# Two block sums of the up weights by an adding load instead of two VectorE additions

## The chip, the cores and the metric

The kernel runs on one core of a Trainium2 chip. The core has five engines with a queue of instructions each: TensorE (PE; its weight loads are listed as PEld), VectorE (DVE), ScalarE (ACT), GpSimd (POOL) and SyncE (SP), which here only issues loads and stores. Semaphores order the engines among each other; the transfers themselves run on 16 DMA engines. The metric is the time of one execution on the device, in microseconds.

## The reference, cut to what matters

Two layers, each with a mixing part (attention, convolution and RWKV heads) and an MLP, on 512 positions of width 1024 in float32. The change touches the MLP alone:

```python
h = rms_norm(x, norm_mlp_g[l])                                        # (512, 1024)
x = x + jnp.square(jax.nn.relu(h @ w_mlp_up[l])) @ w_mlp_down[l]      # up 1024 -> 4096, down 4096 -> 1024
```

## The kernel before

**Layout.** All activations lie transposed: `x[j]` is a tile of 128 features by 512 positions, j from 0 to 7. Weights lie in device memory as groups of 128 output columns, each a row of 8 blocks of 128x128; half a group, four blocks, is 128x512 floats, 256 KB, and is what one load brings.

**Precision.** Float32 products are made of three matmuls: each operand is split into a high part (a cast to `fp32r`, on ACT) and a low part (operand less high part, on DVE or POOL), and high x high, high x low and low x high are added in PSUM. So every weight block that goes into a matmul costs one cast and one subtraction first.

**The up products.** The 32 groups of up columns are treated in two ways. The first four (`N_ONE`) go one by one through `up`: eight blocks, 24 matmuls of 512 positions. Three of the four are written into the order by hand that ends the mixing part (`products`, under `manual_schedule`). The other 28 are taken in pairs (`two(i0, i1)`, 14 pairs a layer): the product of a 2x2 block matrix (two groups by two halves of the 1024 features) with a 2x2 block matrix of activations (two halves of the features by two halves of the positions, H = 256) is made with seven block products instead of eight, after Winograd. With w11, w12 the halves of group i0 and w21, w22 those of group i1, the weights of the seven products p1 to p7 are w11, w12, s4 = w12 - s2, w22, s1 = w21 + w22, s2 = s1 - w11 and s3 = w11 - w21. Each product is four blocks, 12 matmuls of 256 positions (`product`); the order on PE is p1, p5, p6, p2, p7, p3, p4. They gather in three PSUM tiles, `pa`, `pb` and `pc`. The activations' own differences are made once a layer by `blocks(q)`, q from 0 to 3, from the activations times gain (`bn`, made by `by_gain`), and split into `thi` and `tlo`.

The block sums are made by `sum_` on DVE from raw loads (`raw`, tag `sraw`, six buffers; SyncE issues them). In the first pair of a layer s1 and s3 are made with a form that also adds a column of zeros (`none`), which holds them back until the last activation is there. `both` casts (ACT) and subtracts (DVE) into five buffers `shi` and `slo`, so that weights can be made up to five products ahead of PE.

**After the products.** PSUM parts are copied or added into `p1`, `p5`, `u2`, `c1`, `c0`. `square` takes the larger of a value and 0 times the norm's factor `rs` (DVE, into a tile `r`), squares it (ACT, into `m`), and `kept` splits `m` into `mh` and `ml`, the inputs of the down products; `ml` is made on POOL from the fifth on. Ten buffers (`RING`) hold them.

**The down products** come in half groups, `down(h, js)`: four output tiles of 12 matmuls of 512 positions each, added into `x` by DVE. One such call follows nearly each pair; between the second and the third pair of a layer there is none. The weights come through `weights`, with four sets of buffers (three in `wp`, one in `fp`).

**Order.** Behind the hand-written order of the mixing part the instructions are placed by a scheduler that goes by the order of the program and by the times that it assumes, with a queue in order for each engine. So a load may be issued well ahead of its place in the text. At the end of the mixing part (`inner_norm`) POOL raises the mean square to -1/2 (L371, `rrf`), PE spreads it over the partitions (`prbf`), and ACT copies it into `rsf`, the factor `rs` of the squares.

At the start of the MLP part the program runs `up(0)` to `up(3)`, `by_gain(0)` to `by_gain(7)`, `down(0, range(4))`, `blocks(0)` to `blocks(3)`, and then the 14 pairs with the other down products. Before the change POOL issues no DMA at all.

Of the kernel before, what the change touches and what calls it, by code (L numbers as in the profile page):

```python
# [22 lines left out]
S = 512  # L23
# [248 lines left out]
def tile_trunk(ctx: ExitStack, tc: tile.TileContext, xT, wts, prm_d, cst_d, lora_d, gup_d, lam_d, fin_d, hd_d, out):  # L272
# [293 lines left out]
    for l in range(L):  # L566
# [826 lines left out]
        with ExitStack() as mx:  # L1393
# [17 lines left out]
            def square(cs, name):  # L1411

                r = fp.tile([P, S], F32, tag="r", bufs=2, name=f"r{name}")
                for i, c in enumerate(cs):
                    q = slice(i * H, i * H + c.shape[1])
                    dve.scalar_tensor_tensor(r[:, q], c, 0.0, rs[:, q], ALU.max, ALU.mult)
                m = fp.tile([P, S], F32, tag="m", bufs=3, name=f"m{name}")
                act.activation(m, r, AF.Square)
                kept(m)
# [26 lines left out]
            def blocks(q):  # L1446
                hi, lo = th[q] = [fp.tile([P, 4, H], F32R, tag=f"t{p}{q}", name=f"t{p}{l}_{q}") for p in ("hi", "lo")]
                for i in range(2):
                    u = slice(2 * i, 2 * i + 2)
                    t = fp.tile([P, 2, H], F32, tag="c0" if q == 1 else ("s3", "s4")[i], bufs=1 + (q == 1), name=f"t{l}_{q}_{i}")  # L1450
                    for k in (2 * i, 2 * i + 1):
                        b1, b2, o = bn[k], bn[k + 4], t[:, k % 2]
                        if q == 0:
                            dve.tensor_tensor(o, b1[:, 1], b1[:, 0], ALU.subtract)
                        elif q == 1:
                            dve.tensor_tensor(o, b2[:, 1], tb[0, i][:, k % 2], ALU.subtract)
                        elif q == 2:
                            dve.tensor_tensor(o, b2[:, 1], b1[:, 1], ALU.subtract)
                        else:
                            dve.tensor_tensor(o, b2[:, 0], tb[1, i][:, k % 2], ALU.subtract)  # L1460
                    tb[q, i] = t
                    act.copy(hi[:, u], t)
                    dve.tensor_tensor(lo[:, u], t, hi[:, u].bitcast(F32), ALU.subtract)

            def two(i0, i1):
# [4 lines left out]
                def raw(i, a):  # L1470
                    t = fp.tile([P, 4, P], F32, tag="sraw", bufs=6, name=f"raw{n}_{i}_{a}")
                    nc.sync.dma_start(t.rearrange("p k c -> p (k c)"), wts[wg + i, :, a * P:(a + 4) * P])
                    return t
# [7 lines left out]
                def sum_(name, a, b, op):  # L1481
                    t = fp.tile([P, 4, P], F32, tag=name, name=f"{name}{n}")
                    if i0 == N_ONE and name in ("s1", "s3"):
                        dve.scalar_tensor_tensor(t, a, none, b, ALU.add, op)
                    else:
                        dve.tensor_tensor(t, a, b, op)
                    return t
# [22 lines left out]
                w21 = raw(i1, 0)  # L1510
                w22 = raw(i1, 4)
                s1 = sum_("s1", w21, w22, ALU.add)
# [3 lines left out]
                s2 = sum_("s2", s1, w11, ALU.subtract)  # L1516
# [3 lines left out]
                w12 = raw(i0, 4)  # L1520
                product(pc, both(w12, "p2"), blk(1, 0))
                dve.tensor_tensor(c0[:, :H], pc, p1, ALU.add)
                s3 = sum_("s3", w11, w21, ALU.subtract)
                product(pa, both(s3, "p7"), smm(2), False)
# [3 lines left out]
                s4 = sum_("s4", w12, s2, ALU.subtract)  # L1528
# [4 lines left out]
                square([pa, c1], f"{n}_1")  # L1533
# [25 lines left out]
            for i in range(N_ONE):  # L1559
                up(i)  # L1560
            for j in range(NK):
                by_gain(j)
# [83 lines left out]
```

## Time and profile before

| what | us |
|---|---|
| three timed runs: lowest, median, highest | 1236.31, 1236.34, 1236.89 |
| the profiled execution | 1238.42 |
| its span, first to last instruction | 1236.6 |
| busy: PE, DVE, ACT, POOL | 1226.2, 934.4, 693.0, 351.7 |

The page lists an instruction group as line, engine, operation, written tile and read tiles, shape, and count; then the busy time and the mean in nanoseconds, and the idle time of the engine ahead of it with what ended it. `L285` is the matmul helper for nearly all products, so a group of PE is told by its tile: `pa`, `pb`, `pc` belong to the pairs, `dn` to the down products, `up` to the single up products, `po` to the output projection that ends the mixing part, `prbf` to the norm. `raw<-wts` are the weight loads. In other views a row begins with its start in microseconds from the start of the span. `SPq` means SyncE's queue. PE's clock was granted in full over the whole span but for its last microseconds.

The MLP part of layer 0 begins at 278.64 us with the first `up` matmul, that of layer 1 just behind 886.5 us, where the last `po` matmul ends.

### The profile page before, as it was taken

How to read it: one execution, taken by the hardware profiler on the slowest of the kernel's cores; microseconds unless marked ns; L12 is line 12 of the kernel's file. 1: busy time of each engine (PE TensorE's matmuls, PEld its weight loads, DVE VectorE, ACT ScalarE, POOL GpSimd, SP SyncE). 2: the span in 40 equal slices, each digit the busy share in tenths (PEclk: the TensorE clock that was granted, in tenths of full speed). 3: DMA queues.
4: the chain of work that ended last, by engine and by line, in shares of the span. 5: the costliest groups of instructions: out<-in, count | busy, mean ns of one | idle time of the engine just before them, and what ended most of it. 6: DMA issues, size and time to landing. Idle time of an engine off the chain costs nothing.

```text
span 1236.6 us, 25555 instructions
## 1 busy us (share of the span) xinstructions
PE 1226.2 (99%) x9730; PEld 1056.4 (85%) x9730; DVE 934.4 (76%) x1805; ACT 693.0 (56%) x1456; POOL 351.7 (28%) x450
## 2 busy tenths in 40 slices
PE   9999999999999999999999999999999999999997
PEld 7788788888999998989888888888889999998987
DVE  6787888879887676765666777887798867676753
ACT  6785655558455454544465657464775545454542
POOL 2263636341122111120035455464202211111111
PEclk9999999999999999999999999999999999999999
DMA  6523323124433323321235243232433333323121
GB/s 217 165 91 96 111 90 111 54 86 154 143 97 102 103 94 107 99 86 44 69 105 166 77 126 114 88 85 70 152 113 118 106 102 102 104 95 107 55 69 68
DMA packets 84266, 127.94 MB, mean 103 GB/s; under 512 B 21296, under 2 KB 25136, under 8 KB 84144
## 3 DMA queue, kind: packets, MB, share of 16 engines
q1 hardware_dynamic: 83424, 125.57, 32.5%
q8 instruction: 76, 1.25, 0.4%
q10 hardware_dynamic: 720, 0.75, 0.2%
q14 instruction: 46, 0.38, 0.1%
HBM read 117.11 MB, written 9.18 MB: 102 GB/s over the span
## 4 chain that ended last, share of the span: by engine, by line
PE 92%; DVE 2%; ACT 2%; DMA 1%; POOL 1%; issue 1%; SPq 0%; POOLq 0%; ACTq 0%; DVEq 0%
PE dn L285 25%; PE pj L285 21%; PE pa L285 13%; PE po L285 8%; PE pb L285 7%; PE dnF L285 4%; PE pc L285 3%; PE up L285 2%; PE sc L285 1%; PE ptt L290 1%; PE pg L285 1%; PE pyy L285 1%; PE pzw L285 1%; PE pst L285 1%; DMA raw<-wts 0%
## 5 line engine op out<-in xcount | busy, mean ns | idle before, releaser
L1408 POOL TENSOR_TENSOR ml<-m,mh 128x512 fp32r<-128x512 f32 x56 | 90.5, 1634 | 497.5 <-ACT mh L1407 356.5
L285 PE MATMUL dn<-mh,whi 128*128 128x512 f32 x448 | 175.5, 392 | 0.0
L285 PE MATMUL dn<-ml,whi 128*128 128x512 f32 x448 | 175.2, 391 | 0.1
L285 PE MATMUL dn<-mh,wlo 128*128 128x512 f32 x448 | 175.2, 391 | 0.0
L692 POOL TENSOR_TENSOR wlo<-raw,whi 128x512 fp32r<-128x512 f32 x84 | 111.5, 1328 | 210.4 <-ACT whi L680 167.2
L346 ACT CAST whi<-raw 128x512 fp32r<-128x512 f32 x126 | 77.9, 619 | 157.5 <-PE dn L285 147.8
L285 PE MATMUL pj<-ahim,whi 128*128 128x512 f32 x392 | 156.8, 400 | 0.0
L285 PE MATMUL pj<-ahim,wlo 128*128 128x512 f32 x392 | 156.4, 399 | 0.0
L285 PE MATMUL pj<-alom,whi 128*128 128x512 f32 x392 | 155.9, 398 | 0.0
L1554 DVE TENSOR_TENSOR x<-dn,x 128x512 f32<-128x512 f32 x108 | 74.5, 690 | 89.9 <-PE dn L285 89.8
L680 ACT CAST whi<-raw 128x512 fp32r<-128x512 f32 x142 | 87.7, 618 | 71.7 <-PE pj L285 27.5
L1477 ACT CAST shi_p<-s 128x512 fp32r<-128x512 f32 x112 | 69.4, 621 | 78.4 <-PE pa L285 61.9
L347 DVE TENSOR_TENSOR wlo<-raw,whi 128x512 fp32r<-128x512 f32 x126 | 97.3, 774 | 6.1 <-ACT whi L346 6.1
L285 PEld LDWEIGHTS dn<-mh,wlo 128*128 128x128 f32 x448 | 84.2, 188 | 18.5
L285 PEld LDWEIGHTS dn<-ml,whi 128*128 128x128 f32 x448 | 84.2, 188 | 17.7 <-DVE ml L1408 0.5
L285 PEld LDWEIGHTS dn<-mh,whi 128*128 128x128 f32 x448 | 84.1, 188 | 17.4
L285 PE MATMUL pa<-thi,shi_p 128*128 128x256 f32 x336 | 95.1, 283 | 0.0
L285 PE MATMUL pa<-tlo,shi_p 128*128 128x256 f32 x336 | 94.9, 282 | 0.0
L285 PE MATMUL pa<-thi,slo_p 128*128 128x256 f32 x336 | 94.1, 280 | 0.0
L1478 DVE TENSOR_TENSOR slo_p<-s,shi_p 128x512 fp32r<-128x512 f32 x112 | 77.6, 697 | 21.2 <-ACT shi_p L1477 18.4
L285 PEld LDWEIGHTS pj<-alom,whi 128*128 128x128 f32 x392 | 73.9, 188 | 14.0 <-issue 0.5
L285 PEld LDWEIGHTS pj<-ahim,wlo 128*128 128x128 f32 x392 | 73.8, 188 | 13.9 <-issue 0.2
(427 smaller groups left out, 3242.5 us busy)
## 6 DMA issues: line engine op xcount, KB each, us to landing
raw<-wts SPq DMA_DIRECT2D x389, 256.0 KB, 2.6
qs<-dqhi SPq DMA_DIRECT2D x24, 128.0 KB, 3.4
ks<-dkhi SPq DMA_DIRECT2D x24, 128.0 KB, 3.6
x<-xT SPq DMA_DIRECT2D x8, 256.0 KB, 5.0
dqhi<-qhi SPq DMA_DIRECT2D x6, 256.0 KB, 3.4
dqlo<-qlo SPq DMA_DIRECT2D x6, 256.0 KB, 3.4
dkhi<-khi SPq DMA_DIRECT2D x6, 256.0 KB, 3.1
dklo<-klo SPq DMA_DIRECT2D x6, 256.0 KB, 3.5
```

The source lines that it names most:

```text
L285: ins = nc.tensor.matmul(*a, **k)
L290: ins = nc.tensor.transpose(*a, **k)
L346: act.copy(hi[:, :n], raw[:, :n])
L347: (pool if a and lean[0] else dve).tensor_tensor(lo[:, :n], raw[:, :n], hi[:, :n].bitcast(F32), ALU.subtract)
L680: yield act.copy(hi[:, k0:k1], raw[:, k0:k1])
L692: yield eng.tensor_tensor(lo[:, k0:k1], raw[:, k0:k1], hi[:, k0:k1].bitcast(F32), ALU.subtract)
L1408: (dve if i < 4 else pool).tensor_tensor(lo, m, hi.bitcast(F32), ALU.subtract)
L1477: act.copy(hi, src)
L1478: dve.tensor_tensor(lo, src, hi.bitcast(F32), ALU.subtract)
L1554: dve.tensor_tensor(x[j], pt, x[j], ALU.add)
```

## The change

- For each pair s1 and s3 come from DMA: a new helper `summed(p, name)` has SyncE load one half group into the tile and POOL issue a second load into the same tile that adds to what is there (`accum_op=ALU.add`). It is called for pair p + 1 in the middle of pair p, and for pair 0 behind `up(3)` and ahead of `by_gain`. The tiles `s1` and `s3` have two buffers each instead of one.
- An adding load can only add, so the signs are arranged for it: s1 = w21 + w22 as before, s3 = w21 + w11, s2 = s1 + w11, s4 = w12 + s2. The differences of the activations in `blocks` change sign to match, for q = 1 and q = 3 with `scalar_tensor_tensor` in place of `tensor_tensor`.
- The second output of a pair comes out with its sign turned; `square` takes the smaller of it and 0 (`ALU.min`), and squaring removes the sign.
- w21 isn't loaded by itself any more. The load buffers `sraw` go from six to five.
- `square` writes into `m` and squares in place; the two tiles `r` go, and `m` has four buffers instead of three.
- `sum_` loses the form with `none`.

```diff
-            def square(cs, name):
-
-                r = fp.tile([P, S], F32, tag="r", bufs=2, name=f"r{name}")
+            def square(cs, name, side=ALU.max):
+
+                m = fp.tile([P, S], F32, tag="m", bufs=4, name=f"m{name}")
                 for i, c in enumerate(cs):
                     q = slice(i * H, i * H + c.shape[1])
-                    dve.scalar_tensor_tensor(r[:, q], c, 0.0, rs[:, q], ALU.max, ALU.mult)
-                m = fp.tile([P, S], F32, tag="m", bufs=3, name=f"m{name}")
-                act.activation(m, r, AF.Square)
+                    dve.scalar_tensor_tensor(m[:, q], c, 0.0, rs[:, q], side, ALU.mult)
+                act.activation(m, m, AF.Square)
                 kept(m)
...
-                    t = fp.tile([P, 2, H], F32, tag="c0" if q == 1 else ("s3", "s4")[i], bufs=1 + (q == 1), name=f"t{l}_{q}_{i}")
+                    tag, bufs = ("c0", 2) if q == 1 else (("s3", 2), ("s4", 1))[i]
+                    t = fp.tile([P, 2, H], F32, tag=tag, bufs=bufs, name=f"t{l}_{q}_{i}")
...
                         if q == 0:
-                            dve.tensor_tensor(o, b1[:, 1], b1[:, 0], ALU.subtract)
+                            dve.tensor_tensor(o, b1[:, 0], b1[:, 1], ALU.subtract)
                         elif q == 1:
-                            dve.tensor_tensor(o, b2[:, 1], tb[0, i][:, k % 2], ALU.subtract)
+                            dve.scalar_tensor_tensor(o, tb[0, i][:, k % 2], -1.0, b2[:, 1], ALU.mult, ALU.subtract)
...
                         else:
-                            dve.tensor_tensor(o, b2[:, 0], tb[1, i][:, k % 2], ALU.subtract)
+                            dve.scalar_tensor_tensor(o, tb[1, i][:, k % 2], -1.0, b2[:, 0], ALU.mult, ALU.subtract)
...
+            sums = {}
+
+            def summed(p, name):
+
+                if p < N_TWO:
+                    i0, i1 = N_ONE + p, N_ONE + N_TWO + p
+                    t = sums[p, name] = fp.tile([P, 4, P], F32, tag=name, bufs=2, name=f"{name}{l}_{i0}")
+                    of = [wts[wbase + NG_IN + NG_OUT + i, :, a * P:(a + 4) * P] for i, a in ((i1, 0), (i1, 4) if name == "s1" else (i0, 0))]
+                    nc.sync.dma_start(t.rearrange("p k c -> p (k c)"), of[0])
+                    pool.dma_start(t.rearrange("p k c -> p (k c)"), of[1], accum_op=ALU.add)
+
             def two(i0, i1):
...
-                    t = fp.tile([P, 4, P], F32, tag="sraw", bufs=6, name=f"raw{n}_{i}_{a}")
+                    t = fp.tile([P, 4, P], F32, tag="sraw", bufs=5, name=f"raw{n}_{i}_{a}")
...
-                    if i0 == N_ONE and name in ("s1", "s3"):
-                        dve.scalar_tensor_tensor(t, a, none, b, ALU.add, op)
-                    else:
-                        dve.tensor_tensor(t, a, b, op)
+                    dve.tensor_tensor(t, a, b, op)
...
-                w21 = raw(i1, 0)
-                w22 = raw(i1, 4)
-                s1 = sum_("s1", w21, w22, ALU.add)
+                s1 = sums[i0 - N_ONE, "s1"]
...
-                s2 = sum_("s2", s1, w11, ALU.subtract)
+                s2 = sum_("s2", s1, w11, ALU.add)
...
                 w12 = raw(i0, 4)
+                w22 = raw(i1, 4)
+                for s in ("s1", "s3"):
+                    summed(i0 - N_ONE + 1, s)
...
-                s3 = sum_("s3", w11, w21, ALU.subtract)
-                product(pa, both(s3, "p7"), smm(2), False)
+                product(pa, both(sums[i0 - N_ONE, "s3"], "p7"), smm(2), False)
...
-                s4 = sum_("s4", w12, s2, ALU.subtract)
+                s4 = sum_("s4", w12, s2, ALU.add)
...
-                square([pa, c1], f"{n}_1")
+                square([pa, c1], f"{n}_1", ALU.min)
...
             for i in range(N_ONE):
                 up(i)
+            for s in ("s1", "s3"):
+                summed(0, s)
             for j in range(NK):
                 by_gain(j)
```

## The prediction

> **What bounds the kernel now.** I read the page first: the busy times, then the chain that ended last by engine.
>
> ```profile
> span 1236.6 us, 25555 instructions
> ...
> PE 1226.2 (99%) x9730; PEld 1056.4 (85%) x9730; DVE 934.4 (76%) x1805; ACT 693.0 (56%) x1456; POOL 351.7 (28%) x450
> ...
> PE 92%; DVE 2%; ACT 2%; DMA 1%; POOL 1%; issue 1%; SPq 0%; POOLq 0%; ACTq 0%; DVEq 0%
> ```
>
> TensorE (PE) is busy for 1226.2 of 1236.6 us and makes 92% of the chain. A busy PE isn't a PE at its peak, so the next view is the chain in order of time, in the stage that the change edits. Columns: start, duration, what, how many matmuls.
>
> ```profile
> 428.77 1.42 PE pa L285 x12
> 430.19 1.44 PE pb L285 x12
> ...
> 437.34 1.43 PE pa L285 x12
> 438.77 11.04 PE dn L285 x48
> 449.81 1.42 PE pa L285 x12
> ```
>
> One period of this stage is a pair of up products (seven products of 12 matmuls, 428.77 to 438.77, 10.00 us) and half a group of down products (48 matmuls, 11.04 us): 21.04 us, and the next pair begins at 449.81, without a gap. The chain consists of PE alone. Three more views say how much room the others have: the waits, the busy times by window (the line ends with clock, DMA share, GB/s), and SyncE's and GpSimd's (POOL's) timelines.
>
> ```profile
> ACT shi_p L1477 <- PE pa L285: 75.7, 99, 1.1
> 420.00:480.00 60.00, 60.00 (x382) 54.36 (x381) 42.79 (x69) 28.50 (x54) 10.06 (x6) 1.00 0.32 102
> 453.96 9.09 SPq L1472 DMA_DIRECT2D raw<-wts  x4
> 462.21 3.35 POOL L1408 TENSOR_TENSOR ml<-m,mh 128x512 fp32r<-128x512 f32 x2 [17.68 <-ACT mh L1407]
> ```
>
> The casts of the weight blocks (shi_p) wait for PE to release a buffer, not for data: everything ahead of PE is early. In 60 us PE is busy for all 60, DVE 42.8, ACT 28.5, POOL 10.1, the DMA engines 32%. So in this stage nothing that makes DVE lighter can make a pair shorter. What is left to win are the places where PE does wait:
>
> ```profile
> 345.61 1.43 PE pb L285 x12
> 347.04 0.59 PE pc L285 x5
> 347.63 1.68 PE pa L285 x12
> ...
> 354.61 11.04 PE dn L285 x48
> 346.90 1.80 DVE L1486 TENSOR_TENSOR s<-raw,raw 128x512 f32<-128x512 f32 x1
> 346.85 3.00 POOL L1408 TENSOR_TENSOR ml<-m,mh 128x512 fp32r<-128x512 f32 x2 [18.50 <-ACT mh L1407]
> 950.71 2.85 PE pa L285 x24
> ...
> 962.56 10.93 PE dn L285 x48
> 913.68 0.62 DVE ml L1408
> 914.34 6.88 PE dn L285 x29
> ```
>
> The third pair of each layer follows the second with no down products between. Its first product begins 1.43 us before 345.61, at 344.18, and its last ends at 354.61: 10.43 us, 0.43 more than 10.00. In layer 1 it is 952.14 (950.71 and half of 2.85) to 962.56: 0.42 more. There a block sum took 1.80 us beside POOL's subtractions. At 914.34 the chain comes to PE from DVE, a stall that I bound by the same 0.4. So at most 0.43 + 0.42 + 0.4 = 1.25 us can be won.
>
> **The change part by part.**
>
> *The two sums leave DVE.* The groups of their lines (count, then min/median/max ns):
>
> ```profile
> L1486 DVE TENSOR_TENSOR s<-raw,raw x52: 680/693/1800, 316.3 to 1153.1; 128x512 f32<-128x512 f32 x52
> L1484 DVE SCALAR_TENSOR_TENSOR s<-raw,none,raw x4: 743/750/1334, 285.0 to 919.9; 128x512 f32<-128x512 f32 x4
> ```
>
> 52 x 0.693 + 4 x 0.750 = 39.0 us of DVE, all 56 of them s1 and s3 of 28 pairs. Of this 0 lies on the path in 26 pairs; in the two dense ones it takes away one of the slow sums, and before 914.34 one sum. I take 0.5 of the 1.25 us: -0.5.
>
> *The loads.* A pair had four loads of 256 KB; now it has w11, w12, w22 and, for each sum, a load and an adding load: 7. With the four of the down weights a period goes from 8 to 11, the DMA share from 0.32 to about 0.44. The pair's own loads land after:
>
> ```profile
> DMA to landing us min/median/max: 2.4/2.6/6.0
> ```
>
> An adding load isn't in this trace. Its transfer I bound by 2.4 and twice 6.0 (it reads what it adds to), and take 5.2, twice the median, since the median is the row of this very form. The sums are asked for a pair ahead, so there is a period, 21 us, or the dense pair's 10 us, for 2.6 + 5.2. Cost 0. If that cover is gone, a late sum stalls PE by what is missing.
>
> *POOL's queue.* Two adding loads a pair stand there, each behind a wait for its plain load; queued behind them are the subtractions ml. In the steady stage POOL has 17.68 us idle before the two ml, and the ml of a pair are read one pair later, so the wait costs 0. In the dense place the ml of 346.85 to 349.85 are read by the down products from 354.61 on: over 4 us of room.
>
> *The issue itself* on POOL isn't in the trace either. Bounds: SyncE's issue, 0.33 us, and POOL's dearest tensor instruction:
>
> ```profile
> L1472 SPq DMA_DIRECT2D raw<-wts x112: 327/328/1362, 279.0 to 1146.5; - x112
> L1408 POOL TENSOR_TENSOR ml<-m,mh 128x512 fp32r<-128x512 f32 x6 | 10.1, 1695 | 53.1 <-ACT mh L1407 35.4 <-PE dn L285 17.7
> ```
>
> so 0.33 to 1.70 us; I take 1.0, between them: the one row is the same kind of instruction, the other the same engine. The Trainium skill, "SBUF — State Buffer", section "SBUF: two separate sides", speaks against such a load: descriptors of a DMA issued on GpSimd can't be written while VectorE holds the port pair that both share in a two-port mode. Its section "Who interferes with whom" leaves out two-input tensor_tensor, which is nearly all that DVE does here; no trace here shows such an issue. If it did hold, each issue could wait out one DVE instruction, an estimate of 0.7 us each, and the entry below would cost some 1.4 us a layer more.
>
> *The entry of the stage* is where the change can cost something, once a layer. The first pair's sums are asked for before the gains, in a burst of loads, and POOL's power (rrf), which PE's broadcast (prbf) needs, is issued in the same microseconds.
>
> ```profile
> 279.05 1.85 SPq L1472 DMA_DIRECT2D raw<-wts  x4
> 282.90 1.46 POOL L371 TENSOR_TENSOR rrf<-rsx,ones 128x4 f32<-128x4 f32 x1 [3.85 <-DVE none L1434]
> 284.98 0.75 DVE L1484 SCALAR_TENSOR_TENSOR s<-raw,none,raw 128x512 f32<-128x512 f32 x1 [0.78 <-DMA raw<-wts]
> 287.36 0.89 PE prbf L285 x8
> 890.75 1.46 POOL L371 TENSOR_TENSOR rrf<-rsx,ones 128x4 f32<-128x4 f32 x1 [3.56 <-DVE none L1434]
> 887.83 5.84 DMA raw<-wts
> 895.29 1.05 PE L285 MATMUL prbf<-cst,rrf 128*128 128x128 f32 x8
> ```
>
> rrf ends at 284.36 and 892.21, so prbf has 3.0 and 3.1 us of room. If both adding loads come ahead of rrf in POOL's queue, the second waits until its plain load has landed (284.98, and 887.83 + 5.84 = 893.67, the times at which the burst's blocks landed), then 0.33 to 1.70 us of issue, then rrf's 1.46: it ends at 286.8 to 288.1 and 895.5 to 896.8. Late by 0 to 0.8 and 0.2 to 1.5: together 0.2 to 2.3 us, or 0 if rrf goes first. I take 0.6, half of the middle, since the order of the queue is open: +0.6.
>
> *Priced at nothing:* s2 and s4 stay one DVE instruction each with another sign. Eight small instructions a layer get the form with a scalar; rows of both forms at 128x256 last 0.42 us. The square writes its first factor into its own tile: same instructions. With five load buffers and three uses a pair a buffer comes back after 1.7 pairs, before it was 1.5. The s3 buffer that the first sum holds during the block differences is matched by the second buffer of that tag.
>
> ```profile
> 340.47 0.69 DVE L1478 TENSOR_TENSOR slo_p<-s,shi_p 128x512 fp32r<-128x512 f32 x1
> 344.99 0.42 DVE L1416 SCALAR_TENSOR_TENSOR r<-pa,rsf 128x256 f32<-128x256 f32 x1
> 339.94 0.42 DVE L1522 TENSOR_TENSOR c<-pc,p 128x256 f32<-128x256 f32 x1 [0.19 <-PE pc L285]
> ```
>
> *Sum:* the profiled execution lasted 1238.42 us, 1236.6 of span and 1.8 around it. 1238.42 - 0.5 + 0.6 = 1238.5. The three timed runs have a median of 1236.34, 2.1 lower; the same +0.1 gives **1236.4 us**: no difference that a measurement of this kernel can tell, for which I take 0.2%, 2.5 us.
>
> **The rivals.**
>
> *A, slower: POOL is held at the entry until an adding load has landed, and rrf stands behind it.* Then rrf ends at 284.98 + 2.6 to 6.0 + 1.46 = 289.0 to 292.4 and 893.67 + the same = 897.7 to 901.1. PE stalls at prbf by 1.7 to 5.1 and 2.4 to 5.8 us. With -0.5 the time is 1239.9 to 1246.7, 1243 in the middle. It decides against me once the two stalls add up to 3 us. For it: SyncE's order shows pair loads issued at 279.05, ahead of work that comes earlier in the program, so POOL's order may be turned likewise. Against: SyncE isn't held by its DMAs, an issue lasts 0.33 us where the landing takes 2.6. Chance 0.20.
>
> *B, slower: the burst at the entry delays the up weights.*
>
> ```profile
> 280.00:290.00 10.00, 10.00 (x62) 8.21 (x62) 8.22 (x17) 8.74 (x15) 2.75 (x2) 1.00 0.87 288
> 288.62 1.29 POOL L692 TENSOR_TENSOR wlo<-raw,whi 128x512 fp32r<-128x512 f32 x1 [4.26 <-PE up L285]
> 288.25 13.86 PE up L285 x61
> ```
>
> At 288 GB/s the DMA engines are 87% busy. Two loads and two adding loads more, 0.91 us each and the adding ones double, are 5.5 us. The last low half of up weights ends at 289.9; 36 matmuls (one and a half of 24) before 302.1 at 13.86/61 = 0.227 us put its use at 293.9: 4.0 us of room. So 1.5 us a layer: 1236.4 + 3.0 = 1239.4. Against: only loads that SyncE issues behind the new ones are late. Chance 0.08.
>
> *C, faster: PE's rate depends on other engines' traffic.* The 48 down matmuls take 11.04 us in layer 0 and 10.93 in layer 1. If DVE's 39 us of reading and writing made such a 1% in all 28 periods of 21.04 us, 589 us, the time would be 1236.4 - 5.9 = 1230.5. Against: DVE does the same in both layers, and the products beside the collision at 345.61 take the same 1.43 us. Chance 0.04. The Trainium skill, "TensorE: Matmul & The Clock Gate", section "Wait — 56ns, not 53.3ns?", gives a warm matmul its columns over 2.4 GHz and 2.5 ns, an estimate of 109 ns for 256 columns; the trace has 1.43/12 = 119. By that rule 10 ns of each of the 84 x 28 matmuls could go, some 23 us, 1213; no run here shows that rate.
>
> *That the sums don't leave DVE* can't be: their lines are gone from the code.
>
> **How the numbers follow.** Forecast 0.68, A 0.20, B 0.08, C 0.04. All of A and B lie over 1238.8 (0.2%), C under 1233.9: faster 0.04, same 0.68, slower 0.28. The range begins at 1235.1 (1.25 won, nothing lost) and goes to 1241.5, over B and the lower quarter of A: what lies outside is C and 0.15 of A, 0.19.
>
> **What would show it.** Right: periods of 21.04 us in the steady stage, casts that still wait for PE, DVE some 39 us less busy, POOL's ml as far ahead of the down products as now, the third pair at 10.0 to 10.4 us. The entry: prbf at 287.4 and 895.3 relative to the last po product, at most some tenths later. Wrong: A shows as idle PE ahead of prbf with rrf behind an adding load; B as idle PE ahead of up with a late wlo; C as matmul groups of the same count that are shorter. The time would be wrong in the other direction, above all, if adding loads took over 10 us each: then every pair would wait.

## The result and the profile after

| | us |
|---|---|
| before, median of the shared runs (lowest to highest) | 1236.32 (1235.73 to 1236.89) |
| after, median of four runs (lowest to highest) | 1244.55 (1242.68 to 1244.79) |
| ratio after/before, 95% interval | 1.0063 (1.0046 to 1.0081) |
| forecast | 1236.4, range 1235.1 to 1241.5 |

The change makes the kernel 8 us slower, and the forecast was wrong: no difference was the likeliest, and the range ends 3 us too low. The profiled execution of after lasted 1242.68 us, of which the span is 1240.9.

First the page of after: busy times, two DMA queues (packets, MB, share of 16 engines), and the issues of the sums' loads (count, KB, median us to landing).

```profile
PE 1226.7 (99%) x9730; PEld 1055.1 (85%) x9730; DVE 889.1 (72%) x1749; ACT 692.2 (56%) x1456; POOL 385.0 (31%) x506
...
q1 hardware_dynamic: 87456, 132.91, 34.9%
q0 software_dynamic: 8064, 14.68, 7.4%
...
s<-wts SPq DMA_DIRECT2D x56, 256.0 KB, 3.4
s<-wts POOLq DMA_DIRECT2D x56, 256.0 KB, 4.9
```

DVE lost the 45 us that the sums took (39.0 by the prediction's medians), and the adding loads land after 4.9 us, near the 5.2 that the prediction took. So these parts are close to their prices; what is wrong lies in how they meet. The chain in order of time, in the steady stage:

```profile
389.20 1.42 PE pa L285 x12
...
399.20 11.04 PE dn L285 x48
410.24 1.42 PE pa L285 x12
```

The period is 410.24 - 389.20 = 21.04 us, as before. From the fourth pair on every period is what it was to a hundredth, 21.04 us in layer 0 and 20.93 in layer 1: nothing was lost there. The entry is left: from the last `po` matmul to the start of the fourth pair. The chain's rows at the two ends in layer 0, for before and then for after:

```profile
259.82 18.81 PE po L285 x83
365.65 1.42 PE pa L285 x12
```

```profile
259.78 17.47 PE po L285 x77
368.16 1.42 PE pa L285 x12
```

365.65 - (259.82 + 18.81) = 87.02 us before, and 368.16 - 277.25 = 90.91 after. With layer 1 (87.00 and 88.51) the two entries take 174.02 us before and 179.42 after, 5.4 more; in a second profile of after they take 182.46, 8.4 more. This sum of both layers is called **the entry sum** below. Between the two single profiles the span grew by 4.3 us (1240.9 against 1236.6), so the whole loss is in it. Inside it, DVE's timeline of after (in brackets the idle time ahead and what ended it):

```profile
282.37 0.43 DVE L1454 TENSOR_TENSOR t<-bn 128x256 f32<-128x256 f32 x1 [0.88 <-ACT bn L1442]
289.31 0.69 DVE L1494 TENSOR_TENSOR s<-s,raw 128x512 f32<-128x512 f32 x1 [6.51 <-DMA s<-wts]
289.92 0.42 DVE L1454 TENSOR_TENSOR t<-bn 128x256 f32<-128x256 f32 x1
...
900.60 0.69 DVE L1494 TENSOR_TENSOR s<-s,raw 128x512 f32<-128x512 f32 x1 [5.23 <-DMA s<-wts]
```

The instruction that waits is s2 of the first pair, s1 + w11. It stands in DVE's queue right behind the first difference of activations, and the s1 that it reads now comes from the adding load. DVE stands still for 6.51 and 5.23 us, and the other fifteen differences, a low half of up weights and the squares of the up products wait behind an instruction whose result PE needs only some 28 us later, in the third product of the first pair (it starts at 315.64, its third product at 318.50). The chain of after in layer 0 goes through it:

```profile
281.83 7.45 DMA s<-wts
...
289.31 0.07 DVE s L1494
...
308.73 6.91 PE dn L285 x29
```

In between it consists of DVE's instructions and the steps from one to the next. (In layer 1 the inferred chain comes to the same stretch of DVE from ACT's `bn`, which ends at 901.16, only 0.05 us ahead of the difference behind s2; there the entry grew by just 1.5 us.) Why the wait costs so much is shown by the windows behind it (us; busy PE, PEld, DVE, ACT, POOL; clock, DMA share, GB/s), before and then after:

```profile
290.00:300.00 10.00, 10.00 (x46) 8.29 (x45) 9.74 (x20) 9.09 (x17) 0.00 (x0) 1.00 0.25 89
300.00:310.00 10.00, 10.00 (x45) 8.19 (x44) 10.00 (x20) 6.37 (x12) 0.00 (x0) 1.00 0.21 73
```

```profile
280.00:290.00 10.00, 10.00 (x62) 8.31 (x61) 2.60 (x8) 7.39 (x12) 2.99 (x3) 1.00 0.94 255
290.00:300.00 10.00, 9.07 (x39) 6.97 (x38) 9.99 (x19) 6.83 (x13) 2.25 (x2) 1.00 0.70 195
300.00:310.00 10.00, 8.16 (x35) 6.14 (x35) 10.00 (x21) 8.34 (x16) 0.00 (x0) 1.00 0.30 98
```

From 290 to 310 DVE is full in both kernels. It is the second bound of this stretch, hidden by a share of 76% over the span. Most of the time that it loses ahead of 290 (2.60 of 10 us busy, before 8.22) isn't made up, and comes out as PE's idle time, for up products and, up to 20 us later, for down products (timeline of PE; in brackets its idle time):

```profile
291.00 0.50 PE L285 MATMUL up<-ahif,wlo 128*128 128x512 f32 x1 [0.71 <-DVE wlo L692]
294.23 0.50 PE L285 MATMUL up<-ahif,wlo 128*128 128x512 f32 x1 [0.22 <-POOL wlo L692]
307.88 0.51 PE L285 MATMUL dn<-mh,whi 128*128 128x512 f32 x1 [1.49 <-ACT mh L1407]
308.73 0.50 PE L285 MATMUL dn<-ml,whi 128*128 128x512 f32 x1 [0.35 <-DVE ml L1408]
```

Counted from start to start of the matmuls, which are 0.227 us apart elsewhere, these four stalls cost 3.9 us, all that the entry of layer 0 grew by.

In the second profile of after the entry of layer 0 is 2.8 us longer still, and only part of that is waiting. The same place has a wait of 1.95 us, up to 308.90, and behind it PE's granted clock falls to 0.57 between 309 and 313 us (it is 1.00 in the windows ahead and behind):

```profile
309.00:313.00 4.00, 3.65 (x9) 2.72 (x10) 3.55 (x8) 2.17 (x4) 0.00 (x0) 0.57 0.52 146
```

Down matmuls start 0.43 us apart there instead of 0.23, which costs 1.5 us in all.

### The profile page after: what moved, and what is told of

The parts are those of the page before. It is cut to its first block, busy times and chain, and to the rows that moved or that the text cites. A ratio compares the mean times of both kernels' runs of the same rounds, so it can differ in the third digit from the quotient of the medians.

```text
span 1240.9 us, 25747 instructions
## 1 busy us (share of the span) xinstructions
PE 1226.7 (99%) x9730; PEld 1055.1 (85%) x9730; DVE 889.1 (72%) x1749; ACT 692.2 (56%) x1456; POOL 385.0 (31%) x506
## 3 DMA queue, kind: packets, MB, share of 16 engines
q1 hardware_dynamic: 87456, 132.91, 34.9%
q0 software_dynamic: 8064, 14.68, 7.4%
## 4 chain that ended last, share of the span: by engine, by line
PE 92%; DVE 3%; ACT 2%; DMA 2%; issue 1%; POOLq 0%; SPq 0%; POOL 0%; ACTq 0%; DVEq 0%
PE dn L285 24%; PE pj L285 22%; PE pa L285 13%; PE po L285 8%; PE pb L285 7%; PE dnF L285 4%; PE pc L285 3%; PE sc L285 1%; PE ptt L290 1%; PE pg L285 1%; DMA s<-wts 1%; PE pyy L285 1%; PE pzw L285 1%; DVE tlo L1463 1%; PE pst L285 1%
## 5 line engine op out<-in xcount | busy, mean ns | idle before, releaser
L1474 POOL DMA_DIRECT2D s<-wts x56 | 50.7, 906 | 368.2 <-DVE slo_p L1489 222.7
L1408 POOL TENSOR_TENSOR ml<-m,mh 128x512 fp32r<-128x512 f32 x56 | 76.8, 1401 | 114.6 <-ACT mh L1407 70.6
L347 DVE TENSOR_TENSOR wlo<-raw,whi 128x512 fp32r<-128x512 f32 x126 | 94.2, 750 | 6.0 <-ACT whi L346 6.0
```

The costliest lines, as they stand in the source:

```text
L347: (pool if a and lean[0] else dve).tensor_tensor(lo[:, :n], raw[:, :n], hi[:, :n].bitcast(F32), ALU.subtract)
L1408: (dve if i < 4 else pool).tensor_tensor(lo, m, hi.bitcast(F32), ALU.subtract)
L1474: pool.dma_start(t.rearrange("p k c -> p (k c)"), of[1], accum_op=ALU.add)
```

## The experiments

Theories, as the expectations name them: **H**, DVE stands still behind s2; **B**, the burst of loads at the entry delays the weights; **A**, POOL's queue is held; **S**, a cost in every pair. Every kernel ran beside the kernel before, whose median was 1236.69, 1237.00, 1236.78, 1236.79 and 1236.77 us in the five groups of runs. An entry sum is that of one profiled execution.

### Is it the wait, the burst or the signs?

s2 of the first pair later in DVE's queue: it takes a column of zeros that is made from a block difference of the second round.

```diff
-                    dve.tensor_tensor(t, a, b, op)
+                    if i0 == N_ONE and name == "s2":
+                        dve.scalar_tensor_tensor(t, a, late, b, ALU.add, op)
...
+                if q == 1:
+                    dve.tensor_scalar(late, th[1][1][:, 3, :1].bitcast(F32), 0.0, None, ALU.mult)
```

> The changed kernel with all its transfers and POOL instructions; only the first pair's s2 in each layer is made with a form that also adds a column of zeros taken from the low part of the second block difference, so that it stands some 18 places later in VectorE's queue. Theory H (VectorE stands still behind s2, which waits for the adding load): the two waits of 6.5 and 5.2 us before s2 go to 0, the stalls of PE at up and at the first down products shrink from 5.1 us in the two entries to under 1.5, and the time is 1236 to 1238. Theory A (POOL's queue is held) and theory B (the burst of loads delays the up weights): both causes are still there, the time stays at 1240 to 1245.

The first pair's sums on DVE, as before the change, adding loads from the second pair on:

```diff
-                s1 = sums[i0 - N_ONE, "s1"]
+                if i0 == N_ONE:
+                    w21 = raw(i1, 0)
+                    w22 = raw(i1, 4)
+                    s1 = sum_("s1", w21, w22, ALU.add)
+                else:
+                    s1 = sums[i0 - N_ONE, "s1"]
...
+                s3 = sum_("s3", w11, w21, ALU.add) if i0 == N_ONE else sums[i0 - N_ONE, "s3"]
...
-            for s in ("s1", "s3"):
-                summed(0, s)
```

> The changed kernel, but the first pair of each layer makes s1 and s3 on VectorE from raw loads, as the kernel before did; adding loads from the second pair on (26 of 28 pairs). H, A and B alike place the loss in the entry and expect 1236 to 1237.5. Theory S (adding loads cost something in the steady stage, by traffic or by POOL's queue) expects 1242 or more, since 26 of 28 pairs are as in the changed kernel.

No adding load at all, all else of the change, six load buffers (`summed` and its calls go):

```diff
-                s1 = sums[i0 - N_ONE, "s1"]
+                w21 = raw(i1, 0)
+                w22 = raw(i1, 4)
+                s1 = sum_("s1", w21, w22, ALU.add)
...
+                s3 = sum_("s3", w11, w21, ALU.add)
```

> The changed kernel without any adding load: all sums on VectorE from raw loads, with the new signs, the squares in place, and six load buffers. H, A, B and S expect the time of the kernel before, 1236.3 within 0.7. Only if the signs, the form with a scalar in the block differences or the squares in place cost something is it slower.

The same with five load buffers, and at each entry two loads and two adding loads that nothing reads:

```diff
+            for i, s in enumerate(("z1", "z3")):
+                t = fp.tile([P, 4, P], F32, tag=s, name=f"{s}{l}")
+                for eng, g, k, add in ((nc.sync, N_ONE + N_TWO, 0, {}), (pool, N_ONE + (1 - i) * N_TWO, 4 * (1 - i), {"accum_op": ALU.add})):
+                    eng.dma_start(...)
```

> The third experiment's kernel, with two plain and two adding loads into tiles that nobody reads, issued at the entry of each layer where the changed kernel asks for the first pair's sums, and with five load buffers. H expects at most 1.5 us more than the third experiment, as no instruction of VectorE waits for an adding load (the first sum may wait longer for its raw loads). A and B expect 3 us more or above, as POOL's queue and the burst are those of the changed kernel's entry.

| kernel | median us | ratio to before (95%) | entry sum |
|---|---|---|---|
| s2 late | 1239.22 | 1.0021 (1.0012 to 1.0030) | 177.13 |
| first pair on DVE | 1237.50 | 1.0005 (0.9997 to 1.0014) | 174.74 |
| signs only | 1236.57 | 0.9998 (0.9989 to 1.0007) | 173.69 |
| burst unread | 1239.88 | 1.0021 (1.0012 to 1.0030) | 175.24 |

S falls: 26 pairs with adding loads cost nothing that shows. The signs, the squaring in place and the new forms cost nothing either. H and B each hold in part, and neither in the size that its expectation had: moving the waiting instruction leaves 2.5 us of the loss of 6.8 to 8.2, and loads that nothing waits for cost 3.2 by the medians (1239.88 against 1236.69), 2.6 by the ratio. (Some 0.7 us of what moving it gives back is the place of the tiles, of which a later group tells: the periods are 21.01 and 20.90 us in that kernel.) The profile of the burst unread is that of its fastest execution, 1238.10 us, and shows only 1.2 to 1.6 us of its cost.

### The wait alone

The first pair's s1 is a plain load alone, so s2 waits for one landing (adding w22 is left out):

```diff
-                    pool.dma_start(..., of[1], accum_op=ALU.add)
+                    if p or name != "s1":
+                        pool.dma_start(..., of[1], accum_op=ALU.add)
```

> The changed kernel, but the first pair's s1 of each layer is a plain load alone (w21; the adding of w22 is left out there, so that pair's sum lacks a term). The block difference s2 that reads it stands at the same place of DVE's queue. H (DVE stands still behind s2 that waits for the adding load): its wait of 6.51 and 5.23 us shrinks to what a plain load of the burst lacks, 0 to 3 us, and the time falls to 1238.5 to 1240. B (the burst delays all weights): one of eight transfers goes, 1244. A (POOL's queue): rrf comes one adding load earlier, the gain is at most its issue of 0.9 us and the wait ahead of it.

The first two pairs on DVE (as above with `i0 < N_ONE + 2`, and `summed` asked for from the second pair on):

> The changed kernel with the sums of the first two pairs of each layer on DVE; adding loads in the other 24 of 28 pairs. H and B: the entry is as in the kernel before, 1236 to 1237.5; s2 in the third pair finds its sum landed, since it was asked for a pair earlier. S (a cost of 0.29 us in every pair with adding loads): 24 x 0.29 = 7.0 us stay, 1243.5.

The changed kernel again: 

> The changed kernel once more beside the others, for a common base: 1243 to 1245 by every theory.

Load and adding load of the first sum go to a tile that nothing reads, and s1 is one more plain load:

```diff
+                    if not p and name == "s1":
+                        t = fp.tile([P, 4, P - 2], F32, tag="z1", bufs=1, name=f"z1{l}")
+                        of = [o[:, :4 * (P - 2)] for o in of]
+                        nc.sync.dma_start(t.rearrange("p k c -> p (k c)"), of[0])
                     pool.dma_start(..., of[1], accum_op=ALU.add)
```

> The changed kernel, but at each entry the first sum's load and adding load fill a tile that nothing reads (252 KB, two columns less), and the first pair's s1 is one more plain load of w21 (w22 is left out of that sum). So POOL's queue is the same and there is one load more in the burst; only what s2 waits for on DVE differs. H (DVE standing still behind s2 is the cost): 1237.4 to 1238.5, as with the first pair's adding load left out (1237.36), and both idle places of DVE ahead of the first s2 are under 3 us. A or B (POOL's issue, the adding transfer's traffic): 1244 or more, since nothing is lighter.

s2 late in the first pair, as above, and in the third (`late3` is made in the second pair):

```diff
                 dve.tensor_tensor(c1, c1, p5, ALU.add)
+                if i0 == N_ONE + 1:
+                    dve.tensor_scalar(late3[0], c1[:, :1], 0.0, None, ALU.mult)
```

> The kernel with the first pair's s2 later in DVE's queue (1239.22 of time), and now the third pair's s2 too: behind the last subtraction of the second pair. All 28 pairs have their adding loads. H: the stall of 1.58 us ahead of the down products in layer 1 goes, 1237 to 1238. If that stall comes from POOL's or SyncE's queue and not from DVE's order: 1239 again.

The adding load of the first pair's s1 issued twice (w22 is in that sum twice):

```diff
+                    for i in range(1 if p or name != "s1" else 2):
                         pool.dma_start(..., of[1], accum_op=ALU.add)
```

> The changed kernel with a second adding load of w22 on the first pair's s1 in each layer (that sum holds w22 twice). s2 waits for the second landing too. H: about one more landing of 4.9 us and an issue of 0.9 us of DVE's time a layer, of which the slack takes nothing more: 2 x 4.9 to 2 x 5.8 us, 1253 to 1256. A and B: one issue and one transfer of 2.2 us more in the burst a layer, 1245 to 1248.

| kernel | median us | ratio to before (95%) | entry sum |
|---|---|---|---|
| s1 one load | 1237.36 | 1.0005 (0.9996 to 1.0014) | 174.27 |
| two pairs on DVE | 1243.07 | 1.0045 (1.0031 to 1.0059) | 180.67 |
| after again | 1243.77 | 1.0055 (1.0043 to 1.0068) | 182.46 |
| sum beside | 1240.37 | 1.0029 (1.0019 to 1.0040) | 176.62 |
| s2 late twice | 1239.04 | 1.0016 (1.0007 to 1.0025) | 176.91 |
| added twice | 1251.85 | 1.0120 (1.0106 to 1.0134) | 187.55 |

One adding load less a layer gives back 6.4 us, more than H expected. The cleaner cut is the sum beside: POOL's queue is the same and the burst is heavier by a load; besides that only what s2 waits for differs. DVE's timeline there:

```profile
283.24 0.69 DVE L1498 TENSOR_TENSOR s<-s,raw 128x512 f32<-128x512 f32 x1 [0.68 <-DMA raw<-wts]
...
895.45 2.67 DVE L1498 TENSOR_TENSOR s<-s,raw 128x512 f32<-128x512 f32 x1 [1.67 <-DMA raw<-wts]
```

Waits of 6.51 and 5.23 us are 0.68 and 1.67, and of the 6.8 us by which after again lies over its kernel before (1243.77 against 1237.00) 3.6 are left (1240.37 against 1236.78): H is worth 3.2 us, not the 6 that its expectation had. (0.5 of the 3.6 is the place of the tiles, as a later group shows: periods of 21.05 and 20.95 us here instead of 21.04 and 20.93 are some 0.5 us over 27 periods. Without it H is worth 3.7 us, and 3.1 are left, near the burst unread's 2.6 to 3.2.) With the adding load twice it goes the other way; DVE, POOL and PE there:

```profile
293.83 0.69 DVE L1495 TENSOR_TENSOR s<-s,raw 128x512 f32<-128x512 f32 x1 [8.16 <-DMA s<-wts]
910.39 0.69 DVE L1495 TENSOR_TENSOR s<-s,raw 128x512 f32<-128x512 f32 x1 [7.05 <-DMA s<-wts]
```

```profile
906.28 0.87 POOL L1475 DMA_DIRECT2D s<-wts  x1 [4.78 <-DMA s<-wts]
906.85 2.84 POOL L692 TENSOR_TENSOR wlo<-raw,whi 128x512 fp32r<-128x512 f32 x2
```

```profile
908.50 0.50 PE L285 MATMUL up<-ahif,wlo 128*128 128x512 f32 x1 [1.40 <-POOL wlo L692]
```

The waits grow to 15.2 us and begin later too: s2 starts 16.7 and 16.3 us behind the last `po` matmul instead of 12.1 and 11.5. The time grows by 8.1 us over after again, a little less than the least that H expected; and part of it comes in another way. In POOL's queue the adding load of the *second* pair waits 4.78 us for its plain load, a low half of up weights (wlo) stands behind it, and PE is idle for 1.40 us on account of it. The changed kernel has this too: its third adding load in layer 0, and wlo behind it, for which PE waited 0.22 us at 294.23, above.

```profile
291.93 0.92 POOL L1474 DMA_DIRECT2D s<-wts  x1 [6.67 <-DMA s<-wts]
292.57 1.61 POOL L692 TENSOR_TENSOR wlo<-raw,whi 128x512 fp32r<-128x512 f32 x1
```

Two pairs on DVE missed by 6 us, at the 1243 that S alone had expected; but its periods are 21.04 and 20.93 us as before, which is against S. It shows H in another place. The chain in order of time:

```profile
313.39 4.96 DMA s<-wts
...
324.37 0.69 DVE s L1497
...
328.52 7.33 PE dn L285 x24
```

Here the third pair's s2 is the one at which DVE stands still (4.85 us ahead of 324.37; in layer 1 3.91 us ahead of 936.58, where the profile names the DMA of the sum as what ended it): its sum takes the buffer that the first pair's s1 held on DVE, so its load starts only at 313.39, and the third pair follows the second without down products between. PE is idle for 2.24 us ahead of 328.52, and behind that its clock falls to 0.50 between 330 and 332 us. With s2 late in the first pair alone the third pair's s2 waits in layer 1 too, 1.95 us, and PE is idle for 1.42 us at 941.21. With both late that wait is gone, but the time stays, 1239.04: in its profile PE is idle for 1.20 us at 971.13, ahead of down products, behind one long DVE instruction beside two of POOL's:

```profile
966.71 3.76 DVE L347 TENSOR_TENSOR wlo<-raw,whi 128x512 fp32r<-128x512 f32 x1 [0.52 <-ACT whi L346]
...
967.05 2.87 POOL L1408 TENSOR_TENSOR ml<-m,mh 128x512 fp32r<-128x512 f32 x2
```

Such a long subtraction, 3.34 us at 937.22, also stands between s2 and the 1.42 us above, so that stall can't be put down to s2 alone. All 28 pairs with adding loads weren't brought down to 1237 to 1238.

### The burst: traffic or POOL?

Signs only with five buffers, and at each entry three plain loads that nothing reads:

```diff
+            for s, g, n in (("z1", N_ONE, P), ("z2", N_ONE + N_TWO, P), ("z3", N_ONE + 1, P - 2)):
+                t = fp.tile([P, 4, n], F32, tag=s, bufs=1, name=f"{s}{l}")
+                nc.sync.dma_start(...)
```

> The kernel with signs only and five load buffers (as with the unread adding loads), but at each entry three plain loads on SyncE's queue into tiles that nothing reads (two of 256 KB, one of 252 KB), none on POOL. B as traffic: three plain transfers are half of two plain and two adding ones (3 of 6 units of 0.9 us), so half of their cost stays, 1238 to 1238.5. If POOL's issue and wait ahead of rrf is the cost: 1236.6.

The same bytes in pieces of 256 bytes, with the sums on DVE and all loads issued by SyncE:

```diff
-                t = fp.tile([P, 4, n], F32, tag=s, bufs=1, name=f"{s}{l}")
+                t = fp.tile([P, 8, n], F32, tag=s, bufs=1, name=f"{s}{l}")
+                nc.sync.dma_start(t, wts[wbase + NG_IN + NG_OUT + g].rearrange("p (c d) -> p c d", d=P)[:, :, :n])
```

> [...] If the DMA engines' time is what the unread adding loads cost: about 1239.5 to 1240, as with them (1239.88), if the pieces do cost twice. If it is POOL's queue: 1237.7 again.

The burst unread, with two loads and two adding loads of 128x8 numbers each:

```diff
-                t = fp.tile([P, 4, P], F32, tag=s, name=f"{s}{l}")
+                t = fp.tile([P, 8], F32, tag=s, name=f"{s}{l}")
```

> As the kernel with two plain and two adding unread loads at each entry (1239.88), but each of only 128x8 numbers, 4 KB instead of 256: POOL's two issues and its wait for the plain load stay, the traffic goes. If POOL's queue is the cost: 1239.5 to 1240, with rrf ending as late. If it is traffic: 1236.6 to 1237.2.

The last two together:

> Sums on DVE; at each entry both the three unread loads in small pieces and the two unread small adding loads on POOL ahead of rrf. If POOL's queue and the traffic together make the 3 us of the unread adding loads: 1239.5 to 1240. If only an adding transfer of full size does: 1237.5 to 1238.3, the sum of what the two cost alone.

The kernel before with an unused tile and nothing else:

```diff
             for i in range(N_ONE):
                 up(i)
+            fp.tile([P, 16], F32, tag="pad2", name=f"pad2_{l}")
```

> The kernel before with nothing but an unused tile of 64 bytes a partition, which moves what is placed behind it. If placement sets PE's rate in the steady stage: periods of 20.89 and 20.87 us as with the two small unread adding loads, and 1236.8 - 1.9 = 1234.9. If the small adding loads did it: periods of 21.04 and 20.93, 1236.8.

The same with 32 numbers instead of 16: 

> The kernel before with an unused tile of 128 bytes a partition. If placement sets the rate, the periods differ from 21.04 and 20.93 again, by at most 0.2 us, in a direction that no run shows yet: 1233 to 1238.5.

| kernel | median us | ratio to before (95%) | entry sum |
|---|---|---|---|
| plain unread | 1237.69 | 1.0003 (0.9994 to 1.0012) | 174.83 |
| small pieces | 1237.75 | 1.0004 (0.9996 to 1.0013) | 175.27 |
| small adds | 1235.47 | 0.9987 (0.9979 to 0.9996) | 174.99 |
| pieces and adds | 1239.53 | 1.0023 (1.0013 to 1.0033) | 175.45 |
| before with 64 bytes | 1233.47 | 0.9974 (0.9965 to 0.9983) | 173.24 |
| before with 128 bytes | 1236.38 | 1.0000 (0.9991 to 1.0009) | 173.55 |

An empty tile of 64 bytes a partition makes the kernel before 3.3 us faster, the fastest of all here. The chain of that kernel, in the steady stage of layer 0, and that of the one with 128 bytes:

```profile
415.29 10.92 PE dn L285 x48
426.21 1.41 PE pa L285 x12
```

```profile
409.58 1.44 PE pc L285 x12
...
415.34 10.91 PE dn L285 x48
```

Down products take 10.92 instead of 11.04 us (128 bytes: 10.91, but 1.44 us for each product of a pair, which took 1.42 to 1.44). PE is busy without a gap in all of them and the clock is full, so with nothing but the place of the tiles changed PE's pace is another. The period with 64 bytes is 20.89 us, that of small adds 20.89 too: its 1235.47 is best read against 1233.47, though from another group of runs, and the small adds cost 2.0 us. The other two have periods of 21.05 and 20.95 us, 0.5 us in all, and plain unread too. Without that, plain unread loses 0.2, small pieces 0.5, and pieces and adds 2.3 us. Small pieces do load the DMA engines as the burst unread does, by the window at the entry of layer 0, of the burst unread and then of small pieces (share 0.77 and 0.79; plain unread had 0.65):

```profile
276.00:296.00 20.00, 19.91 (x104) 16.11 (x103) 16.15 (x29) 16.18 (x27) 5.54 (x5) 1.00 0.77 226
```

```profile
276.00:296.00 20.00, 20.00 (x107) 16.48 (x106) 16.23 (x30) 17.31 (x29) 3.18 (x3) 1.00 0.79 223
```

By the medians, then, a busy DMA alone isn't the price, and most of it comes with the loads and adding loads of the sums, large or small. The entry sums don't bear this out: over signs only (173.69) plain unread has 1.1 us more, small pieces 1.6, burst unread 1.6, pieces and adds 1.8, and small adds have 1.8 more than 64 bytes (173.24). So which part of the burst is dear isn't shown. DVE's rows at the entry of layer 0, of before with 64 bytes and of small adds, show one way in which it could reach PE:

```profile
283.37 0.75 DVE L1484 SCALAR_TENSOR_TENSOR s<-raw,none,raw 128x512 f32<-128x512 f32 x1 [0.94 <-DMA raw<-wts]
```

```profile
287.27 1.65 DVE L1484 SCALAR_TENSOR_TENSOR s<-raw,none,raw 128x512 f32<-128x512 f32 x1 [2.29 <-DMA raw<-wts]
```

A block that the first pair's sum needs lands later, and DVE stands still behind that sum: like H, with a plain load at the head of DVE's queue. But over both layers these waits are 2.08 us with 64 bytes, 2.29 in small adds, 1.86 in pieces and adds, and 3.24 in the kernel before, which has no burst; so they alone don't make the price. POOL's hold on rrf is small: in small adds rrf ends at 281.37 + 1.98 = 283.35 and PE doesn't wait for prbf, and in the burst unread, with rrf behind both adding loads, PE waits for 0.09 us. What makes the block late, the DMA engines or the order in which SyncE issues it behind the new loads, isn't settled either.

### What holds the third pair at 10.43 us?

In the third pair of each layer the copy of p1 goes from ACT to DVE; once with the first pair's sums on DVE, once with signs only:

```diff
-                act.copy(p1, pa)
+                if i0 == N_ONE + 2:
+                    dve.tensor_copy(p1, pa)
+                else:
+                    act.copy(p1, pa)
```

> Sums of the first pair of each layer on DVE (1237.5), and in the third pair of each layer the copy of the first product's partial sum (p1) from PSUM moves from ACT to DVE. If ACT's late copy is what makes the third pair 10.44 instead of 10.00 us: the third pair takes 10.0 to 10.1 us in both layers and the time falls by 0.4 to 0.9, to 1236.6 to 1237.1, within the measurement's reach of no change. If the block sum's slowness beside POOL was the cause there: 10.44 stays.

> The kernel with signs only (1236.57; no adding load, all block sums on DVE), and in the third pair of each layer the copy of p1 on DVE instead of ACT. If ACT's late copy alone makes the third pair 10.43 us: 10.0 us and 0.4 to 0.9 us less, 1235.7 to 1236.2. If DVE's sum beside POOL makes it long as well: some of the 0.43 stays in each layer.

1236.79 us, ratio 1.0001 (0.9992 to 1.0010), against 1237.50 with the copy on ACT, and 1238.01, ratio 1.0009 (1.0001 to 1.0018), against 1236.57. First PE's weight loads in after, where the third pair still takes 10.44 us; then the chain with the copy moved in the first kernel and in the second:

```profile
350.11 0.19 PEld L285 LDWEIGHTS pa<-thi,shi_p 128*128 128x128 f32 x1 [0.18 <-ACT p L1517]
```

```profile
345.78 1.44 PE pa L285 x12
347.22 1.42 PE pc L285 x12
```

```profile
351.44 2.32 PE dn L285 x10
...
353.77 1.35 DVE m L1416 x3
...
357.59 5.74 PE dn L285 x24
```

In both kernels the third pair now takes 10.0 us, so ACT's copy was the cause and not the slow block sum. Where the sums are on DVE, though, DVE comes late with the squares after it, and PE is idle for 0.59 and 0.68 us in the down products (ahead of 357.59 and 967.26), more than was won. With the sums taken off DVE the gain stays, though the two intervals overlap.

## Why the prediction was wrong, by its steps

- **The failed step** is the first sentence of "Priced at nothing": s2 and s4 stay one DVE instruction each with another sign. Their duration stayed (0.69 us). But s2 of the first pair got a new thing to wait for, and the prediction asked only what stands behind the waiting instruction on POOL's queue, not on DVE's. It stood ahead of most of DVE's work for the entry. Likewise "a period, 21 us, or the dense pair's 10 us" of cover, with cost 0, holds for every pair but the first, whose sum has no pair ahead of it. Sum beside shows the wait alone to be worth 3.2 us, 3.7 without placement; added twice makes it longer and the time grows.
- The second part of the failure is **rival B**, which had a chance of 0.08. Its price, 1.5 us a layer, 3.0 in all, was near the 2.6 to 3.2 that the burst unread costs, but by luck: it was to reach PE by late up weights, and in the profile of the burst unread PE waits for none. There it waits for a late DVE in layer 1 (`ml`, 0.42 us) and for prbf in layer 0 (0.09 us). The sentence against B, that only loads issued behind the new ones are late, didn't rule it out: blocks that DVE's sums need are among those. How the burst costs what it does stays open.
- **Why the range was missed:** the wait's 3.7 us and the 3.1 left beside it are together the 6.8 us by which after again is slower (8.2 in the first runs). That is one difference taken apart; the only measurement of the second part by itself is the burst unread. The first part was not among the cases, and the second alone would have lain within the range. Part of the first is the fall of PE's clock behind the longest stall, 1.5 us where it was seen, which had no place in the prediction either. And the prediction read DVE as 76% busy over the span and 43 of 60 us in the steady stage; the windows from 290 to 310, where DVE is full, weren't read.
- **Steady stage, 0:** right. Periods unchanged with 45 us less on DVE, and adding loads of 4.9 us are hidden. The DMA share rose to 0.50 from 390 to 450 us, not 0.44, since the 11 loads of a period were counted alike: q0 moved 14.68 MB in 7.4% of the engines' time, q1 132.91 MB in 34.9%, so a MB of adding load takes 1.9 times that of a plain one, the double that B's working used.
- **-0.5 for the dense pairs:** wrong. They lasted 10.44 and 10.43 us as before, since ACT's copy of p1 held them and not the slow block sum.
- **+0.6 for rrf:** the order came as assumed, two adding loads ahead of it (POOL's rows in after, below), and the issue is 0.87 to 1.06 us, as taken. But the second plain load had landed early enough: rrf ended at 283.89 + 1.36 = 285.25, and PE didn't wait. The term is 0.
- **A:** POOL isn't held by the landing of an adding load, yet by that of a *plain* load ahead of the next adding load, with wlo behind it instead of rrf: PE is idle for 0.22 us in after, more where the adding load was doubled.
- **C:** falls, the pairs and down products didn't change with DVE's load. The difference of 11.04 and 10.93 that it rested on is of the kind that placement makes.

```profile
281.83 1.06 POOL L1474 DMA_DIRECT2D s<-wts  x1 [4.18 <-DMA s<-wts]
283.33 0.87 POOL L1474 DMA_DIRECT2D s<-wts  x1 [0.43 <-DMA s<-wts]
283.89 1.36 POOL L371 TENSOR_TENSOR rrf<-rsx,ones 128x4 f32<-128x4 f32 x1
```

The issues of 56 adding loads lasted 0.85 to 1.24 us, median 0.88, beside a DVE that was busy most of the time. The wait of an estimated 0.7 us each, which the prediction drew from the Trainium skill, "SBUF — State Buffer", section "SBUF: two separate sides", doesn't show, in line with its section "Who interferes with whom", which has two-input tensor_tensor take only the read side of the shared ports, marked there as inferred.

## What to carry to other kernels

When a result moves from an engine to a DMA, look up every instruction that reads it in its engine's queue, and ask what stands behind that instruction, not only whether the data is early on average; the first use after an entry is where it isn't. Read the windows of each stage for a second engine that is full there: most of the time lost on it ahead of that stretch can come back as a stall, here up to 20 us later. Before a difference of a few tenths of a per cent is put down to a wait, compare the periods of a stage that has none, and the granted clock behind a stall: placement alone moved this kernel by 0.26%.

## What had not been expected of the hardware

- An unused tile of 64 bytes a partition made 48 down products of layer 0 10.92 instead of 11.04 us and the kernel before 3.3 us faster (ratio 0.9974, 0.9965 to 0.9983); 128 bytes did not (1.0000). Which tile's place matters wasn't looked into, nor whether the changed kernel gains as much.
- PE's clock falls behind a stall of about 2 us: in three of the 20 profiles (after again, added twice, two pairs on DVE) it is 0.50 in the middle of a stretch of some 3.4 us that begins 0.4 to 1.6 us behind a wait of 1.94 to 2.24 us. Behind 1.49 us (after) and 2.76 us (added twice, layer 1) it stayed full, so which stalls bring it about isn't known.
- One DVE subtraction of 128x512, otherwise 0.68 us, lasted 3.76 us while POOL made two subtractions in 2.87 us. The Trainium skill, "SBUF — State Buffer", section "Who interferes with whom", says that a DVE instruction with two inputs in SBUF contends with a POOL instruction that reads SBUF; the trace agrees, and 0.68 + 2.87 = 3.55 is near a full wait. It isn't one case: the low half of a block of down weights (`wlo`, line L347) takes 2.6 to 3.9 us on DVE one to four times in each of the ten profiles with adding loads in the pairs, after among them, always beside two `ml` on POOL, and never over 1.8 us in the other ten. Most of the time PE doesn't wait for it.
